# Narrow 4-byte products for the gate weights, a 128-row broadcast of the running maximum, and a layer-2 modulation whose sums are the stationary operand

## The chip, the cores and the metric

One core of one Trainium2 chip runs the whole program. The metric is the device time of one execution in microseconds (us). Engines are named as in the profile: PE is TensorE's matmul side and PEld its weight loads, DVE is VectorE, ACT is ScalarE, POOL is GpSimd, SP is SyncE, which issues the DMAs. PSUM is the accumulator memory, with eight banks.

## What is computed

Two layers over 512 tokens of 1024 channels. Cut to what the change touches:

```
mod = silu(c) @ w_ada[l] + b_ada[l]; shift, scale, gate = split(mod, 3)
h = rms_norm(x, norm_g) * (1 + scale) + shift;   u = h @ w_in
rg_x, rg_z, ml_x, ml_o, ml_z = split(u)
y_rg = rglru(conv(rg_x)) * silu(rg_z)
xc = silu(conv(ml_x)); q = xc @ w_q; k = xc @ w_k; v = ml_x @ w_v      # 4 heads of 256 channels
gates = [q, k, v] @ w_if + b_if      # 3072 x 8: log i and f of 4 heads
s = (q k^T / 16) * exp(d - m_t), causal;  m_t a running maximum over tokens
cell = s v / max(|sum s|, exp(-m_t));    y_ml = norm(sigmoid(ml_o) * cell) * silu(ml_z)
x = x + gate * ([y_rg, y_ml] @ w_out)
```

Everything is in 4-byte floats, and the answer is wanted to that precision.

## The kernel before, in words

**Products.** A large product is made of three: each operand is split into a rounded part (`whi`, `hh`, `xch`, ...; ACT writes it, type fp32r) and the rest (`wlo`, `hl`, `xcl`, ...; DVE writes it), and `mm3` (line 495) adds high x high, high x low and low x high in a PSUM bank. An fp32r product is one record on PE. A product of unsplit 4-byte operands (`f32=True`) is two records of the same shape on PE.

**Order.** The class `Planner` records every instruction and then issues each engine's in the order of a list schedule with its own costs; PE follows the traced order except where an operand isn't there yet in its plan, and then takes a later product. Each engine then runs its list strictly in order. The SBUF tiles come from slots: three for raw weights (`raw`), four each for their two parts (`whi`, `wlo`), 62 others.

**One layer.** First the conv inputs of the heads (`mx`, lines 1199 to 1248), then for each head `qk_weights` (line 781), once `v_gate_weights` (line 801), and `ml_head` (line 838): `p = A x` with `A = w_q w_k^T`, `v`, and the scores `S`. The gates' columns are never made from q, k and v: `w_if` is multiplied into `w_q`, `w_k`, `w_v` beforehand, and the 8 result columns ride along as extra columns of `p` (512 to 520) and of `v` (256 to 264). Then `gate_chain` (line 906) makes the running maximum, and for each head `ml_oz`, `ml_sw` (line 980), `ml_sv`, `ml_yt`; then the RG-LRU half, and `w_out` (`out`, `outq`).

**The gate weights before.** `gate_weights` pads the 8 columns of each block of `w_if` to 32. `qk_weights` runs four unsplit products with the padded block as stationary operand (128 x 32) and 256 columns of raw weights moving, each in another quarter of the array's columns (`tile_position=(0, 32q)`), into one bank `wqg`. `fold` (line 770) copies the bank to SBUF (`wfsb`), transposes and adds the quarters by two unsplit products with a selector (`wfT`), and copies the result (`wf`). `v_gate_weights` does the same with the bank `wvg` for `w_v`, two heads at a time, on raw weights: `w_vT` is not split.

**The modulation of layer 2** (the program's `l = 1`). DVE sums the products over the eight row blocks into `macc` (128 x 1024 in two tiles), in the background. `mod_sum` (line 645) then adds over the 128 rows: four tiled products with a block of ones as stationary operand and 256 columns of `macc` moving (`modps`), a copy (`modsb`), and two products with `sel4` that turn the row into columns (`modT`).

**The maximum.** `mhl` holds the four rows of the running maximum in two parts, in rows 0 to 3 and 32 to 35; `ml_sw` spreads one head's row over 128 partitions by a product with `selh` over 36 rows (`Mbc`).

Of the kernel before, what the change touches and what calls it, by code (L numbers as in the profile page):

```python
# [15 lines left out]
ALU = mybir.AluOpType  # L16
# [14 lines left out]
# columns of the packed per-channel parameters  # L31
# [3 lines left out]
# what of adaLN is summed up on the vector engine: (layer, third)  # L35
# [3 lines left out]
# order of the rows of w_out: the mLSTM half first  # L39
CORD = list(range(8, 16)) + list(range(0, 8))  # L40
# where block j of the causal scores lies: (tile, first column)
# [4 lines left out]
class View:  # L46
    """A part of a logical tile; becomes an access pattern when its instruction is issued."""
# [60 lines left out]
class Planner:  # L108
    """Records instructions, then issues them on each engine in the order of a list schedule: the tensor
    engine follows the traced order, the others serve what it needs first."""  # L110
# [132 lines left out]
    def deadlines(self):  # L243
# [14 lines left out]
        # a PSUM bank is wanted again by a later tile; ready a little ahead of that  # L258
# [27 lines left out]
    def schedule(self):  # L286
# [4 lines left out]
        ready = {e: [] for e in engines}     # (late, i)  # L291
        events = []                          # (time, i): a finished instruction
        nfree = {k: [(0.0, s) for s in range(n)] for k, (n, _) in self.kinds.items()}
        # tiles still without a slot, by the deadline of their first use
# [18 lines left out]
        def fits(o):  # L313
# [4 lines left out]
            for k, bs in need.items():  # L318
                room = len(nfree[k]) - len(bs)
                if room < 0:  # L320
                    return False
                # slots stay for the tiles that come before these
                ahead, w, h, last = 0, want[k], head[k], max(b.first for b in bs)
                while h < len(w) and w[h][0] < last:
                    if w[h][1].slot is None and w[h][1] not in bs:
                        ahead += 1
                        if ahead > room:
                            return False
                    h += 1
            return True  # L330

        def bank_free(o):
            # engines take turns at a PSUM bank
# [24 lines left out]
        while done < len(ops):  # L358
# [23 lines left out]
            # next time at which something changes  # L382
# [43 lines left out]
def trunk_kernel(ctx: ExitStack, tc: tile.TileContext, x, cT, params, bif, bgate, fg,  # L426
# [80 lines left out]
    # t < s: above any maximum, so that its exponential is 0; elsewhere below any  # L507
# [3 lines left out]
    # rows 32 q of four row groups; and pairs of groups, or all, row by row  # L511
    sel4, sel2, selg = keep("sel4", [128, 4]), keep("sel2", [128, 2]), keep("selg", [128, 16])
    sela, selm, selh = keep("sela", [128, 8]), keep("selm", [36, 4]), keep("selh", [36, 4, 128], F32R)

    def selectors():
        P.vcopy(sel4, ident[:, 0:128:32])
        P.tt(sel2, ident[:, 0:128:64], ident[:, 32:128:64], ALU.add)
        for n in range(2):
            P.tt(selg[:, 8 * n:8 * n + 8], ident[:, 64 * n:64 * n + 8], ident[:, 64 * n + 32:64 * n + 40], ALU.add)
        P.tt(sela, selg[:, 0:8], selg[:, 8:16], ALU.add)  # L520
        P.tt(selm, ident[0:36, 0:4], ident[0:36, 32:36], ALU.add)
# [32 lines left out]
    def log1p_exp_neg(ab, shape):  # L554
        # log(1 + exp(-ab)) for ab >= 0: u = exp(-ab), 2 atanh(u / (2 + u))
# [23 lines left out]
    # 4 softplus(-lambda), and halves of the biases of the RG-LRU gates, for both layers  # L579
# [18 lines left out]
    def mod_first(d0, nd):  # L598
        # shift and scale of the first layer, channel blocks d0 .. d0 + nd
# [5 lines left out]
        for k in range(4):  # L605
            # quadrants: (which, half of the rows)
# [25 lines left out]
    def mod_units(l, w):  # L632
        # third w (shift, scale, gate) of layer l: products and sums over the blocks of rows, one step a block
# [11 lines left out]
    def mod_sum(l, w):  # L645
        # the sum over the rows of a block
# [14 lines left out]
        ps = bank("modps", (128, 256))  # L661
        for q in range(4):
            P.mm(ps[32 * q:32 * q + 32, :], ones[:, 0:32], acc[q // 2][:, 256 * (q % 2):256 * (q % 2) + 256], True,
                 True, tp=(0, 32 * q), f32=True)
        sb = slot("modsb", F32, (128, 256))
        P.vcopy(sb, ps)
        pt = bank("modT", (128, 4, 2))
        for c in range(2):
            P.mm(pt[:, :, c], sb[:, 128 * c:128 * c + 128], sel4, True, True, f32=True)
        pt = pt.chan(KC)  # L670
# [32 lines left out]
    def h_part(l, hT, xn, d0, nd, half):  # L703
        # channel blocks d0 .. d0 + nd of two token blocks, transposed, scaled, shifted, split
# [48 lines left out]
    def silu2(ps, name, shape=(128, 512)):  # L753
        # 2 silu
# [6 lines left out]
    def gate_weights(l):  # L761
        raw = slot("wifraw", F32, (128, 24, 8))
        P.dma(raw, w_if[l], 98304)
        pad = [slot("wifpad", F32, (128, 16, 32)), slot("wifpadv", F32, (128, 8, 32))]
        for t, a, b in ((pad[0], 0, 16), (pad[1], 16, 24)):
            P.pool(lambda t=t: nc_g.memset(t.ap(), 0.0), [t], [], 0.4)
            P.vcopy(t[:, :, 0:8], raw[:, a:b, :])
        return pad

    def fold(ps, sel, n):  # L770
        # rows 32 q + g of ps, transposed and summed over the groups q that sel joins: [128, chunk, n]
        sb = slot("wfsb", F32, (128, 256))
        P.vcopy(sb, ps)
        pt = bank("wfT", (128, 2, n))
        for c in range(2):
            P.mm(pt[:, c, :], sb[:, 128 * c:128 * c + 128], sel, True, True, f32=True)
        t = P.tile("gw", (128, 2, n), F32, "wf")
        P.vcopy(t, pt)
        return t

    def qk_weights(l, p, st):
        # A = w_q w_k^T, and the gates' weights seen through w_q and w_k
        raw = load_raw(w_qk[l, p], (2, 2, 256))
        ps = bank("wqg", (128, 256))
        for m in range(2):
            for ec in range(2):
                q = 2 * m + ec
                P.mm(ps[32 * q:32 * q + 32, :], st["pad"][0][:, 8 * m + 2 * p + ec, :], raw[:, m, ec, :], True, True,
                     tp=(0, 32 * q), f32=True)
        hi, lo = load_w(None, (2, 2, 256), raw)  # L790
        pa = bank("A", (128, 2, 256))
        for dc in range(2):
            ds = slice(128 * dc, 128 * dc + 128)
            for ec in range(2):
                mm3(pa[:, dc, :], hi[:, 0, ec, ds], lo[:, 0, ec, ds], hi[:, 1, ec, :], lo[:, 1, ec, :], ec == 0, ec == 1)
        ah, al = slot("Ah", F32R, (128, 2, 256)), slot("Al", F32R, (128, 2, 256))
        split(ah, al, pa)
        st["A"][p] = (ah, al)
        st["gq"][p] = fold(ps, sela, 8)

    def v_gate_weights(l, st):
        for u in range(2):
            raw = load_raw(w_vT[l, u], (2, 2, 256))
            ps = bank("wvg", (128, 256))
            for h in range(2):
                for ec in range(2):
                    q = 2 * h + ec
                    P.mm(ps[32 * q:32 * q + 32, :], st["pad"][1][:, 2 * (2 * u + h) + ec, :], raw[:, h, ec, :],
                         True, True, tp=(0, 32 * q), f32=True)
            st["gv"][u] = fold(ps, selg, 16)  # L810

    def v_weights(l, u, st):
        # w_v of two heads, with the gates' columns beside it
# [581 lines left out]
```

## Time and profile before

| | |
|---|---|
| time, median of 3 runs | 856.05 us (855.46 to 856.55) |
| span of the profiled execution | 853.5 us, 12548 instructions |
| the profiled execution's own time | not listed apart from its span; the median lies 2.5 us above that span |
| PE busy | 835.0 us, 98% |
| DVE, ACT, POOL busy | 607.3, 476.7 and 40.9 us |
| DMA | 107.60 MB, 126 GB/s on the mean |

The span runs from the first to the last instruction of the core. A matmul's busy time overlaps the next one's, so the cost of a matmul in a dense stream is the distance from its start to the next start, not its duration. In the views, "128\*32" is the stationary operand's rows and columns, and "128x256" the moving one.

### The profile page before, as it was taken

The numbers are of one execution on the slowest core, as the hardware profiler recorded it, in microseconds if no ns is written. First come the engines' busy times: TensorE is split into PE (matmuls) and PEld (weight loads), VectorE is DVE, ScalarE is ACT, GpSimd is POOL, SyncE is SP. The second block draws the span as 40 slices with busy tenths as digits, with TensorE's granted clock in tenths as the row PEclk, the third lists the DMA queues.
The fourth block names the chain that finished last, engine by engine and source line by source line (L and its number), as shares of the span: only waits on it lengthen the run. The fifth ranks groups of instructions, "written<-read, shape, count | busy, mean of one in ns | idle before, by whom it ended". The sixth has DMA issues, their size and how long they took to land.

```text
span 853.5 us, 12548 instructions
## 1 busy us (share of the span) xinstructions
PE 835.0 (98%) x4664; PEld 698.1 (82%) x4664; DVE 607.3 (71%) x1227; ACT 476.7 (56%) x938; POOL 40.9 (5%) x66
## 2 busy tenths in 40 slices
PE   4999999999999999999999999999999999999996
PEld 3677897888888888887999789878888888888896
DVE  5467976898889699654466897376775877967643
ACT  4357763655457969622146766364454696893322
POOL 3000001011100000000010000100000000000000
PEclk9999999999999999999999999999999999999999
DMA  9924132466553323523231422033333222273202
GB/s 323 323 81 137 62 121 78 149 202 210 183 195 111 112 74 125 196 99 123 88 107 62 159 87 99 26 111 136 125 109 122 91 77 96 70 252 123 74 26 99
DMA packets 37053, 107.60 MB, mean 126 GB/s; under 512 B 4352, under 2 KB 6400, under 8 KB 36992
## 3 DMA queue, kind: packets, MB, share of 16 engines
q1 hardware_dynamic: 36992, 106.80, 36.2%
q8 instruction: 37, 0.61, 0.3%
q14 instruction: 24, 0.20, 0.1%
HBM read 102.58 MB, written 4.19 MB: 125 GB/s over the span
## 4 chain that ended last, share of the span: by engine, by line
PE 97%; DVE 1%; DMA 1%; POOL 1%; SPq 0%; ACT 0%; issue 0%; POOLq 0%
PE oz L153 20%; PE mx L153 11%; PE outq L153 11%; PE out L153 11%; PE rgz L153 10%; PE rgx L153 10%; PE S L153 4%; PE num L153 3%; PE v L153 3%; PE p L153 3%; PE A L153 2%; PE modps L153 2%; PE px L153 1%; PE pa L153 1%; PE hT L162 1%; PE yT L162 1%
## 5 line engine op out<-in xcount | busy, mean ns | idle before, releaser
L183 ACT CAST whi<-raw 128x1024 fp32r<-128x1024 f32 (+1 forms) x133 | 130.9, 994 | 186.7 <-PE oz L153 63.1
L190 DVE TENSOR_TENSOR wlo<-raw,whi 128x1024 fp32r<-128x1024 f32 (+1 forms) x133 | 151.9, 1148 | 72.4 <-ACT whi L183 72.0
L153 PE MATMUL oz<-whi,hh 128*128 128x512 f32 x256 | 101.8, 399 | 0.0
L153 PE MATMUL oz<-whi,hl 128*128 128x512 f32 x256 | 101.2, 395 | 0.0
L153 PE MATMUL oz<-wlo,hh 128*128 128x512 f32 x256 | 101.1, 395 | 0.0
L153 PE MATMUL outq<-whi,yh 128*128 128x256 f32 x256 | 72.5, 283 | 0.0
L153 PE MATMUL outq<-wlo,yh 128*128 128x256 f32 x256 | 72.4, 283 | 0.0
L153 PE MATMUL outq<-whi,yl 128*128 128x256 f32 x256 | 72.4, 283 | 0.0
L153 PE MATMUL mx<-hh,whi 128*128 128x512 f32 (+1 forms) x166 | 59.1, 358 | 0.0
L153 PE MATMUL mx<-hl,whi 128*128 128x512 f32 (+1 forms) x166 | 58.4, 352 | 0.0
L153 PE MATMUL mx<-hh,wlo 128*128 128x512 f32 (+1 forms) x166 | 57.4, 348 | 0.0
L153 PEld LDWEIGHTS oz<-whi,hh 128*128 128x128 f32 x256 | 48.1, 188 | 11.2 <-issue 1.0
L153 PEld LDWEIGHTS oz<-whi,hl 128*128 128x128 f32 x256 | 48.1, 188 | 11.1
L153 PEld LDWEIGHTS oz<-wlo,hh 128*128 128x128 f32 x256 | 48.1, 188 | 10.2
L153 PE MATMUL out<-whi,yh 128*128 128x512 f32 x128 | 50.6, 396 | 0.0
L153 PE MATMUL out<-whi,yl 128*128 128x512 f32 x128 | 50.6, 395 | 0.0
L153 PE MATMUL rgx<-hh,whi 128*128 128x512 f32 x128 | 50.5, 395 | 0.0
L153 PE MATMUL out<-wlo,yh 128*128 128x512 f32 x128 | 50.5, 394 | 0.0
L153 PE MATMUL rgz<-hh,whi 128*128 128x512 f32 x128 | 50.4, 394 | 0.0
L153 PE MATMUL rgz<-hl,whi 128*128 128x512 f32 x128 | 50.4, 394 | 0.0
L153 PE MATMUL rgx<-hl,whi 128*128 128x512 f32 x128 | 50.4, 394 | 0.0
L153 PE MATMUL rgz<-hh,wlo 128*128 128x512 f32 x128 | 50.4, 394 | 0.0
(256 smaller groups left out, 2029.7 us busy)
## 6 DMA issues: line engine op xcount, KB each, us to landing
raw<-in_w_in_dram SPq DMA_DIRECT2D x45, 512.0 KB, 3.2
raw<-in_w_oz_dram SPq DMA_DIRECT2D x32, 512.0 KB, 3.2
raw<-in_w_ada_dram SPq DMA_DIRECT2D x32, 512.0 KB, 3.3
raw<-in_w_out_dram SPq DMA_DIRECT2D x32, 512.0 KB, 3.2
wada<-in_w_adb_dram SPq DMA_DIRECT2D x24, 256.0 KB, 5.2
x<-in_x_dram SPq DMA_DIRECT2D x16, 256.0 KB, 5.5
raw<-in_w_qk_dram SPq DMA_DIRECT2D x8, 512.0 KB, 3.2
wada<-in_w_ada_dram SPq DMA_DIRECT2D x8, 256.0 KB, 4.3
```

What stands on the lines that cost most here:

```text
L153: self.nc.tensor.matmul(out.ap(), lhsT=lhsT.ap(), rhs=rhs.ap(), start=start, stop=stop, **kw)
L162: self.op("PE", lambda: self.nc.tensor.transpose(out.ap(), in_.ap(), ident.ap()), [out], [in_, ident], 0.109)
L183: self.op("ACT", lambda: self.nc.scalar.copy(out.ap(), in_.ap()), [out], [in_], 0.1 + 0.00084 * in_.n)
L190: self.op(eng, lambda: e.tensor_tensor(out=out.ap(), in0=a.ap(), in1=b.ap(), op=op), [out], [a, b], c)
```

## The change

Three edits; comments are removed as well.

1. **Gate weights.** `w_if` is split into `gatew` (8 high and 8 low columns per block). `qk_weights` puts `gatew`'s columns for `w_q` beside the high part of `w_k` (256 to 272 columns), so that they ride along in the products for `A`, and adds for `w_k` eight narrow products per head: `whi` or `wlo` of `w_k` as stationary 128 x 128 operand and 16 or 8 columns of `gatew` moving. `A` now takes two banks of 272 columns, evacuated one by one. `v_gate_weights` splits `w_vT` into two parts and runs 16 narrow products for each pair of heads. `fold`, its selectors and the padding go.
2. **Layer-2 modulation.** `mod_sum` takes 128 x 128 blocks of `macc` as stationary operand and one column of ones as moving one: eight unsplit products a sum, straight into channel layout.
3. **Maximum.** `selm`, `selh` and `mhl` have 128 rows, and `Mbc` is a product over all of them.

```diff
     def selectors():
-        P.vcopy(sel4, ident[:, 0:128:32])
         P.tt(sel2, ident[:, 0:128:64], ident[:, 32:128:64], ALU.add)
-        for n in range(2):
-            P.tt(selg[:, 8 * n:8 * n + 8], ident[:, 64 * n:64 * n + 8], ident[:, 64 * n + 32:64 * n + 40], ALU.add)
-        P.tt(sela, selg[:, 0:8], selg[:, 8:16], ALU.add)
-        P.tt(selm, ident[0:36, 0:4], ident[0:36, 32:36], ALU.add)
+        P.tt(selm, ident[:, 0:4], ident[:, 32:36], ALU.add)
         P.vcopy(selh, selm.spread(2, 128))
...
     def mod_sum(l, w):
-        ps = bank("modps", (128, 256))
-        for q in range(4):
-            P.mm(ps[32 * q:32 * q + 32, :], ones[:, 0:32], acc[q // 2][:, 256 * (q % 2):256 * (q % 2) + 256], True,
-                 True, tp=(0, 32 * q), f32=True)
-        sb = slot("modsb", F32, (128, 256))
-        P.vcopy(sb, ps)
-        pt = bank("modT", (128, 4, 2))
-        for c in range(2):
-            P.mm(pt[:, :, c], sb[:, 128 * c:128 * c + 128], sel4, True, True, f32=True)
-        pt = pt.chan(KC)
+        pt = bank("modT", (128, KC))
+        for c in range(KC):
+            P.mm(pt[:, c:c + 1], acc[c // 4][:, 128 * (c % 4):128 * (c % 4) + 128], ones[:, 0:1], True, True, f32=True)
...
-    def gate_weights(l):
+    def gate_weights(l, st):
...
+        gw = slot("gatew", F32R, (128, 24, 16))
+        split(gw[:, :, 0:8], gw[:, :, 8:16], raw)
+        st["gw"] = gw
...
     def qk_weights(l, p, st):
         raw = load_raw(w_qk[l, p], (2, 2, 256))
-        ps = bank("wqg", (128, 256))
-        for m in range(2):
-            for ec in range(2):
-                q = 2 * m + ec
-                P.mm(ps[32 * q:32 * q + 32, :], st["pad"][0][:, 8 * m + 2 * p + ec, :], raw[:, m, ec, :], True, True,
-                     tp=(0, 32 * q), f32=True)
-        hi, lo = load_w(None, (2, 2, 256), raw)
-        pa = bank("A", (128, 2, 256))
+        hi = P.tile("whi", (128, 2, 2, 272), F32R, "whi")
+        lo = P.tile("wlo", (128, 2, 2, 256), F32R, "wlo")
+        split(hi[:, :, :, 0:256], lo, raw)
+        gw = st["gw"]
+        P.acopy(hi[:, 1, :, 256:272], gw[:, 2 * p:2 * p + 2, :])
...
         for dc in range(2):
+            pa = bank("A", (128, 272))
             ds = slice(128 * dc, 128 * dc + 128)
             for ec in range(2):
-                mm3(pa[:, dc, :], hi[:, 0, ec, ds], lo[:, 0, ec, ds], hi[:, 1, ec, :], lo[:, 1, ec, :], ec == 0, ec == 1)
-        split(ah, al, pa)
+                P.mm(pa, hi[:, 0, ec, ds], hi[:, 1, ec, :], ec == 0, False)
+                P.mm(pa[:, 0:256], hi[:, 0, ec, ds], lo[:, 1, ec, :], False, False)
+                P.mm(pa[:, 0:264], lo[:, 0, ec, ds], hi[:, 1, ec, 0:264], False, False)
+            for ec in range(2):
+                c = 8 + 2 * p + ec
+                P.mm(pa[:, 256:272], hi[:, 1, ec, ds], gw[:, c, :], False, False)
+                P.mm(pa[:, 256:264], lo[:, 1, ec, ds], gw[:, c, 0:8], False, ec == 1)
+            split(ah[:, dc, :], al[:, dc, :], pa[:, 0:256])
+            P.vcopy(gq[:, dc, :], pa[:, 264:272])
+            P.tt(gq[:, dc, :], gq[:, dc, :], pa[:, 256:264], ALU.add)
-        st["gq"][p] = fold(ps, sela, 8)
+        st["gq"][p] = gq
...
     def v_gate_weights(l, st):
         for u in range(2):
-            raw = load_raw(w_vT[l, u], (2, 2, 256))
-            ps = bank("wvg", (128, 256))
+            wh, wl = load_w(w_vT[l, u], (2, 2, 256))
+            pv = bank("wvg", (128, 2, 2, 16))
             for h in range(2):
-                for ec in range(2):
-                    q = 2 * h + ec
-                    P.mm(ps[32 * q:32 * q + 32, :], st["pad"][1][:, 2 * (2 * u + h) + ec, :], raw[:, h, ec, :],
-                         True, True, tp=(0, 32 * q), f32=True)
-            st["gv"][u] = fold(ps, selg, 16)
+                for dc in range(2):
+                    ds = slice(128 * dc, 128 * dc + 128)
+                    for ec in range(2):
+                        c = 16 + 2 * (2 * u + h) + ec
+                        P.mm(pv[:, dc, h, :], wh[:, h, ec, ds], st["gw"][:, c, :], h + dc + ec == 0, False)
+                        P.mm(pv[:, dc, h, 0:8], wl[:, h, ec, ds], st["gw"][:, c, 0:8], False, h + dc + ec == 3)
+            gv = P.tile("gw", (128, 2, 2, 8), F32, "gv")
+            P.vcopy(gv, pv[:, :, :, 8:16])
+            P.tt(gv, gv, pv[:, :, :, 0:8], ALU.add)
...
-        P.pool(lambda: nc_g.memset(mhl.ap()[0:36, :].bitcast(F32), 0.0), [mhl[0:36, :]], [], 0.3)
+        P.pool(lambda: nc_g.memset(mhl.ap().bitcast(F32), 0.0), [mhl], [], 0.5)
...
-        P.mm(pm, selh[:, h, :], st["mrow"][0:36, :], True, True)
+        P.mm(pm, selh[:, h, :], st["mrow"], True, True)
```

Since the planner decides the order, here are three places as the engines are given it. First PE in layer 1 (`l = 0`), right behind the last `mx` product: `wqg` and `wvg` are the tiled gate products, `A` the products of `w_q w_k^T`, `wfT` the fold. Before:

```order
L153 MATMUL A<-whi 128x256
L153 MATMUL wvg<-raw,wifpadv 32x256
L153 MATMUL A<-wlo,whi 128x256
L153 MATMUL wvg<-raw,wifpadv 32x256
L153 MATMUL A<-whi,wlo 128x256
L153 MATMUL wvg<-raw,wifpadv 32x256 x2
L153 MATMUL wfT<-sela,wfsb 128x8 x2
L153 MATMUL wqg<-raw,wifpad 32x256 x4
```

and now, with `gatew` the split gate columns:

```order
L153 MATMUL A<-whi 128x272
L153 MATMUL A<-wlo,whi 128x256
L153 MATMUL A<-whi,wlo 128x264
L153 MATMUL A<-whi 128x272
L153 MATMUL A<-wlo,whi 128x256
L153 MATMUL A<-whi,wlo 128x264
L153 MATMUL A<-gatew,whi 128x16
L153 MATMUL A<-gatew,wlo 128x8
L153 MATMUL A<-gatew,whi 128x16
L153 MATMUL A<-gatew,wlo 128x8
```

The tiled products that stood between the products for `A` are gone, and the narrow ones follow in runs of four (sixteen for `wvg`), all of them over the whole array.

Second DVE at the same place, with its waits; `mconv`, `msilut`, `xcl` and `xml` lead to the operands of `p` and `v`. Before:

```order
L213 COPY wfsb<-wqg 128x256 [waits PE_49]
L190 TENSOR_TENSOR xml<-xmf,xmh 128x512 [waits Activation_49]
L198 SCALAR_TENSOR_TENSOR msilut<-msilut,mconv 128x512 [waits Activation_49]
L213 COPY wfsb<-wvg 128x256 [waits PE_49]
L213 COPY wf<-wfT 128x16 [waits PE_49]
L198 SCALAR_TENSOR_TENSOR msilut<-msilut,mconv 128x512 [waits Activation_49]
L190 TENSOR_TENSOR Al<-A,Ah 128x512 [waits Activation_49]
```

and now:

```order
L190 TENSOR_TENSOR wlo<-raw,whi 128x1024 [waits DMAHW5_49,PE_49,Activation_49]
L198 SCALAR_TENSOR_TENSOR mconv<-xmf,par,mconv 128x511 [waits Activation_49]
L190 TENSOR_TENSOR wlo<-raw,whi 128x1024 [waits DMAHW6_49,PE_49,Activation_49]
L198 SCALAR_TENSOR_TENSOR mconv<-xmf,par,mconv 128x510 [waits DVE_49]
L198 SCALAR_TENSOR_TENSOR msilut<-msilut,mconv 128x512 [waits Activation_49]
L198 SCALAR_TENSOR_TENSOR mconv<-xmf,par,mconv 128x509 [waits DVE_49]
L190 TENSOR_TENSOR Al<-A,Ah 128x256 [waits Activation_49]
L213 COPY gq<-A 128x8
L190 TENSOR_TENSOR Al<-A,Ah 128x256 [waits Activation_49]
```

The copies that waited for the tiled products have gone from the front of the `msilut` steps, and low halves of whole weight tiles (1024 columns) stand among them.

Third PE in the first of the two modulation sums, under the last `w_out` products. Before:

```order
L153 MATMUL modps<-macc,ones 32x256
L153 MATMUL out<-whi,yh 128x512
L153 MATMUL modps<-macc,ones 32x256 x2
L153 MATMUL out<-wlo,yh 128x512
L153 MATMUL modps<-macc,ones 32x256
L153 MATMUL out<-whi,yl 128x512
```

and now:

```order
L153 MATMUL out<-wlo,yh 128x512
L153 MATMUL out<-whi,yl 128x512
L153 MATMUL modT<-ones,macc 128x1 x8
L153 MATMUL outq<-whi,yh 128x256
L153 MATMUL outq<-wlo,yh 128x256
```

Eight products in one run stand where four tiled ones stood in three places, with the two of `modT` further on.

## Rows read from the trace of the kernel before

**Rows 1.** The profile's page: busy time, share and instructions of each engine, the granted TensorE clock in 40 slices (tenths of full speed, 9 is 90% or more), and the chain that ended last by engine.

```profile
PE 835.0 (98%) x4664; PEld 698.1 (82%) x4664; DVE 607.3 (71%) x1227; ACT 476.7 (56%) x938; POOL 40.9 (5%) x66
...
PEclk9999999999999999999999999999999999999999
...
PE 97%; DVE 1%; DMA 1%; POOL 1%; SPq 0%; ACT 0%; issue 0%; POOLq 0%
```

**Rows 2.** The waits of PE, the longest and the shortest of the four there are: who waited for whom, us in total, times, longest.

```profile
PE modps L153 <- DVE hb L206: 4.5, 1, 4.5
...
PE cumb L153 <- DVE lf L198: 1.1, 1, 1.1
```

**Rows 3.** The timeline of PE at the isolated gate products of head 2 in layer 1: start us, busy us, then engine, line, operation, tiles (x8: eight records).

```profile
84.74 0.28 PE L153 MATMUL S<-ph,xcl 128*128 128x264 f32 x1
84.95 0.64 PE L153 MATMUL wqg<-raw,wifpad 128*32 128x256 f32 x8
85.52 0.39 PE L153 MATMUL A<-whi 128*128 128x256 f32 x1
85.75 0.28 PE L153 MATMUL A<-wlo,whi 128*128 128x256 f32 x1
...
87.53 0.39 PE L153 MATMUL mx<-hh,wlo 128*128 128x512 f32 x1
87.76 0.51 PE L153 MATMUL wfT<-sela,wfsb 128*128 128x8 f32 x4
88.12 0.48 PE L153 MATMUL mx<-hh,whi 128*128 128x512 f32 x1
88.44 0.39 PE L153 MATMUL mx<-hl,whi 128*128 128x512 f32 x1
```

**Rows 4.** The chain of work, two dense pieces, of products of 512 and of 256 columns: start us, length us, what, number of products.

```profile
756.32 39.02 PE out L153 x168
...
801.84 45.26 PE outq L153 x384
```

**Rows 5.** The timeline of PE, first and last row of the gate products in layer 1 (between them 24 products of `A`, the `p` rows at 74.70 (two), 75.26 and 75.85, and 48 gate records) and in layer 2 (12 of `A`, the `mx` rows of 512 columns at 472.72, 473.06, 473.28 and 474.32, and 36 gate records).

```profile
64.47 0.39 PE L153 MATMUL mx<-hh,wlo 128*128 128x512 f32 x1
...
76.17 0.40 PE L153 MATMUL p<-xch,Ah 128*128 128x512 f32 x1
...
465.69 0.28 PE L153 MATMUL mx<-hh,wlo 128*128 128x256 f32 x1
...
474.64 0.39 PE L153 MATMUL mx<-hl,whi 128*128 128x512 f32 x1
```

**Rows 6.** The timeline of PE at a run of six products of 136 columns.

```profile
105.00 0.23 PE L153 MATMUL S<-ph,xch 128*128 128x136 f32 x1
105.06 0.27 PE L153 MATMUL S<-pl,xch 128*128 128x136 f32 x1
...
105.62 0.33 PE L153 MATMUL S<-ph,xch 128*128 128x264 f32 x1
105.79 0.28 PE L153 MATMUL S<-pl,xch 128*128 128x264 f32 x1
```

**Rows 7.** The timeline of PE around the two modulation sums: the first and last row of each stretch (between them, in the first, three more products of 512 and nine of 256 columns that stay; in the second, eleven of 256).

```profile
387.09 0.40 PE L153 MATMUL out<-whi,yl 128*128 128x512 f32 x1
...
391.88 0.27 PE L153 MATMUL outq<-wlo,yh 128*128 128x256 f32 x1
...
401.20 0.28 PE L153 MATMUL outq<-whi,yl 128*128 128x256 f32 x1
...
406.05 0.28 PE L153 MATMUL outq<-whi,yl 128*128 128x256 f32 x1
```

**Rows 8.** The timeline of PE at the first broadcast of the maximum, a product over 36 rows.

```profile
147.61 0.40 PE L153 MATMUL oz<-whi,hl 128*128 128x512 f32 x1
147.94 0.50 PE L153 MATMUL Mbc<-mhl,selh 36*128 36x512 f32 x1
148.36 0.50 PE L153 MATMUL oz<-whi,hh 128*128 128x512 f32 x1
148.70 0.39 PE L153 MATMUL oz<-wlo,hh 128*128 128x512 f32 x1
```

**Rows 9.** Busy time by stretch: us, then PE, PEld, DVE, ACT and POOL busy (instructions), granted clock, DMA share, GB/s.

```profile
64.00:76.00 12.00, 12.00 (x80) 7.36 (x79) 7.50 (x16) 7.90 (x16) 0.10 (x1) 1.00 0.44 136
76.00:108.00 32.00, 32.00 (x200) 28.44 (x201) 30.87 (x57) 25.45 (x66) 0.10 (x1) 1.00 0.23 82
```

**Rows 10.** The timelines of ACT and DVE ahead of and in the first gate stretch; in brackets the idle time before the row and what ended it.

```profile
59.15 1.05 ACT L183 CAST whi<-raw 128x1024 fp32r<-128x1024 f32 x1
...
67.17 0.42 DVE L213 COPY wfsb<-wqg 128x256 f32<-128x256 f32 x1 [1.65 <-PE wqg L153]
...
70.61 0.42 DVE L213 COPY wfsb<-wvg 128x256 f32<-128x256 f32 x1 [1.81 <-PE wvg L153]
71.14 0.17 DVE L213 COPY wf<-wfT 128x16 f32<-128x16 f32 x1
...
71.83 0.68 DVE L190 TENSOR_TENSOR Al<-A,Ah 128x512 fp32r<-128x512 f32 x1
...
78.80 1.22 DVE L190 TENSOR_TENSOR wlo<-raw,whi 128x1024 fp32r<-128x1024 f32 x1
...
80.53 0.41 DVE L190 TENSOR_TENSOR vl<-v,vh 128x256 fp32r<-128x256 f32 x1
```

More of the change, by code (lines that the diff above doesn't have):

```diff
@@ L510, in trunk_kernel @@
                                       fill=1e30, base=0, channel_multiplier=-1), [upper], [upper], 0.3)
-    sel4, sel2, selg = keep("sel4", [128, 4]), keep("sel2", [128, 2]), keep("selg", [128, 16])
-    sela, selm, selh = keep("sela", [128, 8]), keep("selm", [36, 4]), keep("selh", [36, 4, 128], F32R)
+    sel2 = keep("sel2", [128, 2])
+    selm, selh = keep("selm", [128, 4]), keep("selh", [128, 4, 128], F32R)
     def selectors():
-        P.vcopy(sel4, ident[:, 0:128:32])
         P.tt(sel2, ident[:, 0:128:64], ident[:, 32:128:64], ALU.add)
-        for n in range(2):
-            P.tt(selg[:, 8 * n:8 * n + 8], ident[:, 64 * n:64 * n + 8], ident[:, 64 * n + 32:64 * n + 40], ALU.add)
-        P.tt(sela, selg[:, 0:8], selg[:, 8:16], ALU.add)
-        P.tt(selm, ident[0:36, 0:4], ident[0:36, 32:36], ALU.add)
+        P.tt(selm, ident[:, 0:4], ident[:, 32:36], ALU.add)
         P.vcopy(selh, selm.spread(2, 128))
@@ L758, in silu2 @@
         return th
-    def gate_weights(l):
+    def gate_weights(l, st):
         raw = slot("wifraw", F32, (128, 24, 8))
         P.dma(raw, w_if[l], 98304)
[L764 to L779, printed above, removed]
+        gw = slot("gatew", F32R, (128, 24, 16))
+        split(gw[:, :, 0:8], gw[:, :, 8:16], raw)
+        st["gw"] = gw
@@ L792, in qk_weights @@
+        lo = P.tile("wlo", (128, 2, 2, 256), F32R, "wlo")
+        split(hi[:, :, :, 0:256], lo, raw)
+        gw = st["gw"]
+        P.acopy(hi[:, 1, :, 256:272], gw[:, 2 * p:2 * p + 2, :])
+        ah, al = slot("Ah", F32R, (128, 2, 256)), slot("Al", F32R, (128, 2, 256))
+        gq = P.tile("gw", (128, 2, 8), F32, "gq")
         for dc in range(2):
+            pa = bank("A", (128, 272))
             ds = slice(128 * dc, 128 * dc + 128)
             for ec in range(2):
-                mm3(pa[:, dc, :], hi[:, 0, ec, ds], lo[:, 0, ec, ds], hi[:, 1, ec, :], lo[:, 1, ec, :], ec == 0, ec == 1)
@@ L796, in qk_weights @@
-        ah, al = slot("Ah", F32R, (128, 2, 256)), slot("Al", F32R, (128, 2, 256))
-        split(ah, al, pa)
+                P.mm(pa, hi[:, 0, ec, ds], hi[:, 1, ec, :], ec == 0, False)
[5 more added lines that the diff above has]
+                P.mm(pa[:, 256:264], lo[:, 1, ec, ds], gw[:, c, 0:8], False, ec == 1)
@@ L812, in v_weights @@
+            gv = P.tile("gw", (128, 2, 2, 8), F32, "gv")
+            P.vcopy(gv, pv[:, :, :, 8:16])
+            P.tt(gv, gv, pv[:, :, :, 0:8], ALU.add)
+            st["gv"][u] = gv
     def v_weights(l, u, st):
@@ L819, in v_weights @@
         for h in range(2):
-            split(hi[:, h, :, 256:264], lo[:, h, :, 256:264], g[:, :, 8 * h:8 * h + 8])
+            split(hi[:, h, :, 256:264], lo[:, h, :, 256:264], g[:, :, h, :])
         st["wv"] = (hi, lo)
@@ L1243, in trunk_kernel @@
             ml_head_pre(l, p, ps01[p], st)
-        st["pad"] = gate_weights(l)
+        gate_weights(l, st)
         qk_weights(l, 0, st)
```

## The prediction

> **What bounds the kernel now.** I read the page first: PE is busy 98% of the span, the chain that ended last is PE for 97%, and the granted clock is at the upper of its two levels (2.4 GHz) in every slice [rows 1]. Then PE's waits: the longest is 4.5 us, at the start of the program, and the shortest is the gate chain's, 1.1 us [rows 2]; in the stretches that the change touches there is none. So every us of PE's own stream there counts in full, and the work of the others counts only where it makes PE wait. Busy time doesn't price a product, since each overlaps the next; I price by the distance between starts. A dense product costs 39.02 / 168 = 0.232 us with 512 columns and 45.26 / 384 = 0.118 us with 256 [rows 4]; one column more is (0.232 - 0.118) / 256 = 0.45 ns.
>
> **What the removed products cost.** Take an isolated group of four tiled gate products [rows 3]. From the score product ahead of it (84.74) to the second product of A (85.75) are 1.01 us. The two products that stay would take 0.121 (264 columns) and 0.118, so the group costs 0.77 us, though its eight records stand only 0.57 us before the next start: the rest is a late start before it and a slow product behind it. There are five such groups (heads 2 and 3 of layer 1, heads 1 to 3 of layer 2): 3.85 us. An isolated fold lies between two mx products: 0.91 us from 87.53 to 88.44, less two products of 0.232, is 0.446 us [rows 3]; five folds, 2.23 us.
>
> In the first gate stretch of each layer the tiled products alternate with products of A, so I take the whole stretch less what stays. Layer 1: 76.17 - 64.47 = 11.70 us, less five products of 512 columns (1.16) and 24 of A (2.83), is 7.71 us. Layer 2: 474.64 - 465.69 = 8.95 us, less 13 products of 256 columns (1.53) and four of 512 (0.93), is 6.49 us [rows 5]. The gate weights cost PE 3.85 + 2.23 + 7.71 + 6.49 = 20.28 us.
>
> **What the narrow products will cost.** There are 64 for the q and k part and 64 for the v part, with 16 or 8 columns moving and a full 128 x 128 stationary operand. No row of before has this shape in fp32r. The nearest is the run of 136 columns: from 105.00 to 105.79 are 0.79 us for six of them and one of 264 (0.121), so 0.112 us each [rows 6]. The unsplit products of the fold, of 8 columns, give the same: 0.446 / 4 = 0.112 a record [rows 3]. At half and at a sixteenth of 136 columns the price doesn't fall, so it is the stationary operand's, and I take 0.112: 128 x 0.112 = 14.34 us. The wider products of A add 32 x 16 and 32 x 8 columns, 0.34 us. The gate weights thus go from 20.28 to 14.68: **-5.6 us**.
>
> The ends: the first of the run is followed after 0.06 us [rows 6], which would take 0.05 from each. Upward, the product behind a run is late by 0.17 - 0.121 = 0.05 us [rows 6]; I have counted that in, but should a run of four pay it once more, it is 0.013 a product, 1.6 us.
>
> The Trainium skill (TensorEngine Tiling (Array Packing), section When to Use Tiling) advises the opposite of this edit: with few moving columns, swap stationary and moving operand and tile the columns, for up to four times the speed. By that, four tiled products take the time of one, which is the price that the slower rival below gives them, and the gate weights would lose 6.5 us by this edit instead of gaining 5.6; the 0.77 us of the rows speak against it. The same page (section Key Properties) says that changing the tiling mode drains the array, and the gaps of these rows agree with that.
>
> **Modulation of layer 2.** First sum: 391.88 - 387.09 = 4.79 us, less four products of 512 (0.93) and ten of 256 columns (1.18), is 2.68 us. Second: 406.05 - 401.20 = 4.85, less twelve of 256 (1.42), is 3.43 us [rows 7]. In their place come 16 unsplit products, two records each: 32 x 0.112 = 3.58 us. Net **-2.5 us**. They need only the sums that the tiled ones needed too; a copy on DVE goes.
>
> **Maximum.** 148.70 - 147.61 = 1.09 us, less two oz products (0.464), leaves 0.63 us for a product that needs 0.232 in a dense stream [rows 8]. All eight read within 0.01 of that, so it is no wait but what goes with 36 rows. With 128 rows I take the plain 0.232: 8 x 0.395 = **-3.2 us**, and as ends no gain and this one. The memset of 128 rows is POOL's, which is 5% busy, and comes well ahead.
>
> **What it puts on ACT and DVE.** Four more weight tiles are split, 1.05 us on ACT and 1.22 on DVE each [rows 10]. Priced at nothing where it is covered; the cover is thin in layer 1. From 64 to 108 us DVE is busy 7.50 + 30.87 = 38.4 of 44 us [rows 9]. That stretch gets shorter on PE: 7.71 + 0.77 + 0.45 go and 56 narrow products (6.27) and 0.13 of width come, -2.5, so 41.5 us. DVE gets two low halves (2.44), six copies and six additions for gq (12 x 0.17, the copy wf as nearest row), four small ones for gv (0.7) and Al in six halves for three wholes (6 x 0.41 - 3 x 0.68 = 0.4), and loses five wfsb (2.1) and five wf (0.85) [rows 10]: 41.0 of 41.5 us. Between 76 and 108 it ran at 96% and PE never waited [rows 9]; at that share 41.0 needs 42.5, a wait of 1 us. In favour: 3.5 us of DVE's idle time were spent behind the copies of wqg and wvg [rows 10], which go, and in the new order the low halves take that place. The middle is 0.5 us; in layer 2 an mx group follows the v part and gives the time back, so with 0.1 for it I take **+0.6 us**, between 0 and 2.5. Late next would be the xcl that p needs, then xml for v. The A products' second bank, one copy of gate columns on ACT per head and the four selector steps that go at the start (PE waits for data there) I price at nothing.
>
> **Sum:** -5.6 - 2.5 - 3.2 + 0.6 = -10.7 us. The profiled execution's span of 853.5 becomes 842.8; the median lies 2.5 us above that span, so I predict **845.4 us**.
>
> **Rivals.**
> *DVE becomes the bound (0.13).* PE waits for xcl or xml in both layers and the front gains go: up to the 5.6 us of the gate weights, 847 to 850.5 us. For it: the 99% above. Against: layer 2 has 48 mx products behind the v part, and the waiting copies go.
> *Narrow products cost their columns (0.06).* If the stationary operand loads under a neighbour, each costs 0.06 us [rows 6]: 160 x 0.05 = 8 us less, 837 to 842. Against: five of the six in that run cost 0.11. The Trainium skill (TensorE: Matmul & The Clock Gate, section Back-to-back issue gap) gives about 25 ns for up to 64 columns; by it the time would be an estimated 831 us. Its section on LDWEIGHTS counts the 128 columns at 1.2 GHz, 107 ns, and the rows agree with that one.
> *The broadcast doesn't gain (0.05).* If the 0.63 us belong to something else than 36 rows, 3.2 us stay: 848.6 us.
> *Slower (0.02): the gaps are not the tiled products' own.* PE's late starts at 64 to 76 and 465 to 476 us would be operands not yet there, which the tiled products only filled. Removing these then frees no more than their passes: twelve groups and 48 fold records, 12 x 2 x 0.118 + 48 x 0.112 = 8.2 us, and for the modulation 2 x 0.236 + 8 x 0.112 = 1.4 us. What comes is 14.7 and 3.6 us: +8.7, less 3.2 for the maximum, and 0.6, makes 862 us. Beyond the passes I count 20.28 + 6.11 - 9.6 = 16.8 us as the tiled products' own; from the point where under 6.1 us of it (36%) are, the change is slower. Against: five groups among different neighbours cost the same to 0.01 us.
>
> **How the numbers follow.** Forecast 842.5 to 847.0 with 0.72, the rivals as above, 0.02 for anything else. The range leaves out about half of the cheap narrow products, the far end of DVE and the slower case: 842.0 to 849.2. A measurement tells 0.2% (1.7 us) from no change. Only the slower rival, and waits for DVE beyond what I bound, reach 856: faster 0.95, same 0.03, slower 0.02.
>
> **What would show it.** Right: records A<-gatew and wvg<-gatew at 0.11 us from start to start; the first gate stretch of layer 1, from the start of the last mx product to that of the first p, at about 8.5 us; modT in two runs of 1.8 us; Mbc followed by the next product after 0.23; PE waits as before but for under 1 us near p or v of layer 1. Wrong: PE waiting for DVE between 64 and 108 us, narrow products at 0.06, or Mbc still at 0.6.

## The result, and the profile after

The changed kernel takes **850.88 us** (median of 4 runs, 850.69 to 852.13), the kernel before beside it 855.75 us (854.86 to 856.55): a ratio of 0.9947, with an interval of 0.9933 to 0.9961. That is 4.9 us faster, where 10.7 us were forecast; 850.88 lies outside the range of 842.0 to 849.2. The profiled execution took 850.69 us, with a span of 849.0 us.

The page of the changed kernel, the rows that answer to [rows 1]:

```profile
PE 829.3 (98%) x4656; PEld 709.6 (84%) x4656; DVE 608.1 (72%) x1247; ACT 481.6 (57%) x960; POOL 40.3 (5%) x62
...
PEclk9998999999999999999999999999999999999999
...
PE 96%; DVE 1%; POOL 1%; DMA 1%; SPq 0%; issue 0%; ACT 0%; POOLq 0%
```

The thing to see is the one 8 in the row of the clock. A slice is 21.2 us long (849.0 / 40), so this slice, from 63.7 to 84.9 us, holds a stretch at less than full clock. In the second layer the dip is too short to move a digit. The waits of PE, answering to [rows 2] (who waited for whom, us in total, times, longest):

```profile
PE modps L153 <- DMA wada<-in_w_ada_dram: 8.5, 2, 5.0
PE hT L162 <- DVE xn L206: 2.4, 1, 2.4
PE cumb L153 <- DVE lf L198: 2.2, 2, 1.1
```

No wait has come near the gate weights, but cumb now waits in both layers, where before it waited in layer 2 alone. The windows of the changed kernel show the clock (columns as in [rows 9]; the clock is the number behind the engines):

```profile
67.00:71.60 4.60, 4.60 (x43) 4.60 (x42) 4.60 (x12) 4.60 (x11) 0.00 (x0) 1.00 0.57 199
71.60:78.50 6.90, 6.90 (x26) 6.13 (x26) 4.50 (x18) 3.97 (x10) 0.10 (x1) 0.51 0.23 76
78.50:84.00 5.50, 5.50 (x45) 5.34 (x44) 4.56 (x8) 4.63 (x13) 0.10 (x1) 1.00 0.11 33
466.00:470.90 4.90, 4.90 (x43) 4.77 (x42) 3.50 (x5) 4.87 (x8) 0.00 (x0) 1.00 0.55 181
470.90:474.50 3.60, 3.60 (x11) 2.77 (x9) 3.60 (x12) 3.60 (x7) 0.00 (x0) 0.53 0.71 240
```

PE is busy in every us of all five, and yet the clock stands at half, its lower level of 1.2 GHz, in the second and the fifth. By the clock records of the trace the lower level lasts from 71.67 to 78.50 us (6.83 us) in layer 1 and from 471.03 to 474.45 us (3.41 us) in layer 2. The timeline of PE shows what stands ahead of it, and the prices:

```profile
64.90 0.39 PE L153 MATMUL mx<-hh,wlo 128*128 128x512 f32 x1
...
67.04 0.17 PE L153 MATMUL A<-gatew,whi 128*128 128x16 f32 x1
...
70.75 0.26 PE L153 MATMUL wvg<-gatew,whi 128*128 128x16 f32 x1
70.86 0.25 PE L153 MATMUL wvg<-gatew,wlo 128*128 128x8 f32 x1
70.97 0.37 PE L153 MATMUL A<-whi 128*128 128x272 f32 x1
...
71.55 0.30 PE L153 MATMUL A<-wlo,whi 128*128 128x256 f32 x1
71.67 0.40 PE L153 MATMUL A<-whi,wlo 128*128 128x264 f32 x1
...
71.93 0.36 PE L153 MATMUL A<-gatew,wlo 128*128 128x8 f32 x1
72.15 0.36 PE L153 MATMUL A<-gatew,whi 128*128 128x16 f32 x1
...
74.75 0.77 PE L153 MATMUL p<-xch,Ah 128*128 128x512 f32 x1
75.32 0.63 PE L153 MATMUL p<-xcl,Ah 128*128 128x512 f32 x1
75.75 0.63 PE L153 MATMUL p<-xch,Al 128*128 128x512 f32 x1
...
149.72 0.40 PE L153 MATMUL Mbc<-mhl,selh 128*128 128x512 f32 x1
149.96 0.40 PE L153 MATMUL oz<-whi,hh 128*128 128x512 f32 x1
...
388.94 1.84 PE L153 MATMUL modT<-ones,macc 128*128 128x1 f32 x16
390.64 0.36 PE L153 MATMUL outq<-whi,yh 128*128 128x256 f32 x1
```

From 67.04 to 70.97 stand 36 narrow products in one unbroken run (four of `A`, 32 of `wvg`): 3.93 us, 0.109 each. Until there the price is what was forecast. At 71.67 the same kind of product that took 0.28 to 0.30 us of busy time takes 0.40; from there a narrow product stands 0.22 us from the next (71.93 to 72.15) and a 512-column one 0.43 (75.32 to 75.75), where [rows 4] have 0.232. In layer 2 the run of 36 ends at 470.07, and the clock falls at 471.03.

### The profile page after: what moved, and what is told of

Same layout as the page of the kernel before. It is cut to its first block, busy times and chain, and to the rows that moved or that the text cites. A ratio compares the mean times of both kernels' runs of the same rounds, so it can differ in the third digit from the quotient of the medians.

```text
span 849.0 us, 12554 instructions
## 1 busy us (share of the span) xinstructions
PE 829.3 (98%) x4656; PEld 709.6 (84%) x4656; DVE 608.1 (72%) x1247; ACT 481.6 (57%) x960; POOL 40.3 (5%) x62
## 4 chain that ended last, share of the span: by engine, by line
PE 96%; DVE 1%; POOL 1%; DMA 1%; SPq 0%; issue 0%; ACT 0%; POOLq 0%
PE oz L153 19%; PE mx L153 11%; PE outq L153 11%; PE out L153 10%; PE rgz L153 10%; PE rgx L153 10%; PE S L153 4%; PE num L153 3%; PE p L153 3%; PE v L153 3%; PE A L153 2%; PE pa L153 1%; PE px L153 1%; PE modps L153 1%; PE hT L162 1%; POOL u L190 1%
## 5 line engine op out<-in xcount | busy, mean ns | idle before, releaser
L183 ACT CAST whi<-raw 128x1024 fp32r<-128x1024 f32 (+1 forms) x137 | 135.2, 996 | 183.1 <-PE oz L153 66.2
L190 DVE TENSOR_TENSOR wlo<-raw,whi 128x1024 fp32r<-128x1024 f32 (+1 forms) x137 | 156.8, 1150 | 75.0 <-ACT whi L183 74.6
```

The costliest lines, as they stand in the source:

```text
L183: self.op("ACT", lambda: self.nc.scalar.copy(out.ap(), in_.ap()), [out], [in_], 0.1 + 0.00084 * in_.n)
L190: self.op(eng, lambda: e.tensor_tensor(out=out.ap(), in0=a.ap(), in1=b.ap(), op=op), [out], [a, b], c)
```

## Experiments

Two questions were open: what lets the clock fall and what it costs, and where the second wait at cumb comes from. The kernel before ran beside each group of experiments, at 855.21 us (e1 to e4), 855.68 (e5 to e8) and 855.65 (e9, e10).

**e1: the narrow products of v made wide.** Same products, same number, same order and same stationary operands; each streams 128 columns, the 16 gate columns eight times, and only the first copy is read.

```
-  pv = bank("wvg", (128, 2, 2, 16))
+  pv = bank("wvg", (128, 2, 2, 8, 16))
...
+  g = st["gw"][:, c, :].spread(1, 8)
-  P.mm(pv[:, dc, h, :], wh[:, h, ec, ds], st["gw"][:, c, :], ...)
+  P.mm(pv[:, dc, h], wh[:, h, ec, ds], g, ...)
-  P.mm(pv[:, dc, h, 0:8], wl[:, h, ec, ds], st["gw"][:, c, 0:8], ...)
+  P.mm(pv[:, dc, h], wl[:, h, ec, ds], g, ...)
```

> The changed kernel with one difference: each of the 64 narrow products of the v part streams 128 columns (its 16 gate columns read eight times over by a broadcast view, into eight copies in the bank, of which one is used) instead of 16 or 8. Same number of products, same order, same stationary operands, and at 0.112 us a product the stationary operand should still set the pace. Theory A (the runs of 32 narrow products leave the array so little active that TensorE's granted clock falls to its lower level behind them, 71.6 to 78.5 and 471.0 to 474.5 us of the changed kernel): the clock stays at 2.4 GHz in both places and about 3.4 + 1.4 = 4.8 us come back, 846 us. Theory B (the clock is beside the point; PE is held by late operands from DVE and ACT in these stretches): 851 us as the changed kernel, with waits of PE for DVE showing at full clock. Theory C (128 columns are dearer than 16): up to 64 x 0.06 = 3.8 us more, 855 us.

Measured: 846.12 us (845.49 to 846.51), ratio 0.9893, 0.9878 to 0.9909; span 843.8 us. The windows of e1, over the run and behind it, and its timeline:

```profile
66.50:70.50 4.00, 4.00 (x39) 4.00 (x37) 4.00 (x9) 4.00 (x10) 0.00 (x0) 1.00 0.63 229
70.50:78.00 7.50, 7.50 (x53) 6.97 (x52) 7.24 (x25) 6.93 (x17) 0.10 (x1) 1.00 0.22 72
```

```profile
64.36 0.39 PE L153 MATMUL mx<-hh,wlo 128*128 128x512 f32 x1
...
69.80 0.27 PE L153 MATMUL wvg<-gatew,whi 128*128 128x128 f32 x1
69.91 0.27 PE L153 MATMUL wvg<-gatew,wlo 128*128 128x128 f32 x1
...
72.79 0.48 PE L153 MATMUL p<-xch,Ah 128*128 128x512 f32 x1
```

With eight or sixteen times the columns a product costs the same 0.11 us, the engines around it are as full, PE runs the same products in the same order, and the clock stays at its upper level. From the last `mx` to the first `p` of layer 1 are 72.79 - 64.36 = 8.43 us, where 8.5 were forecast; in the changed kernel they are 74.75 - 64.90 = 9.85. Between the two profiled executions lie 849.0 - 843.8 = 5.2 us, and half of the 10.24 us at the lower level (6.83 + 3.41) is 5.1: within 0.1 us the difference is the clock.

**e2: the run cut in two.** The second unit of `v_gate_weights` is called later, in each layer behind the last `ml_head_pre`, so that the runs are of 20 and of 16.

```
-  v_gate_weights(l, st)
+  v_gate_weights(l, st, (0,))
...
   ml_head_pre(l, 3, chan_group(l, 11, hT, ("mx0", "mx1")), st)
+  v_gate_weights(l, st, (1,))
```

> The changed kernel with the v part's 32 narrow products of a layer in two runs of 16: those of heads 0 and 1 where they were, those of heads 2 and 3 behind the mx products of head 3 (layer 1) or likewise behind them in layer 2. No product is added or taken. Theory A (clock): if the run's length matters, the clock falls for a shorter time or not at all, 846 to 849 us; PE waits for nothing more. Theory B (late operands): two of the four extra weight splits move out of the dense stretch of DVE, so it gains too, but with the clock still low behind the runs: 848 to 851 us. What tells them apart is the granted clock beside the time.

Measured: 847.16 us (847.09 to 848.98), ratio 0.9909, 0.9896 to 0.9923; span 845.4 us. The windows of e2, with the first run of 20 in layer 1 (67.73 to 69.88) and in layer 2 (462.73 to 464.88), and behind each:

```profile
66.50:70.00 3.50, 3.50 (x33) 3.50 (x33) 3.50 (x7) 3.50 (x8) 0.00 (x0) 1.00 0.48 150
70.00:77.00 7.00, 7.00 (x49) 6.47 (x49) 6.45 (x23) 6.28 (x15) 0.10 (x1) 1.00 0.24 78
```

```profile
461.50:464.80 3.30, 3.30 (x32) 3.30 (x30) 3.25 (x5) 3.27 (x5) 0.00 (x0) 1.00 0.53 169
464.90:468.30 3.40, 3.40 (x10) 2.72 (x10) 2.67 (x6) 3.40 (x8) 0.00 (x0) 0.50 0.43 140
```

Half the cure: in the profiled execution the fall of layer 1 is gone, that of layer 2 is there with its 3.41 us. In one of the four executions the mean clock was 0.994 and not 0.997, and the time 848.98 us where the others took 847.09 to 847.18. Cutting the run is not a safe remedy, then. Why one run of 20 is followed by a fall and the other isn't, no run here tells. No fall followed a run of 16 in any trace, neither the second runs of e2 nor the modulation's 16 records of one column.

**e3: v's gate weights as before, the rest changed.** `v_gate_weights`, its padded tile and its fold come back from the kernel before; q and k keep the narrow products, in groups of four (once two groups in a row).

> The changed kernel with the v part of the gate weights as it was before (tiled products on raw weights, fold), the q and k part narrow. Theory A: no run of more than 4 narrow products is left, the clock stays up, which gives 4.8 us; the v part costs about 4.6 us a layer (four tiled products in islands among A, four together, two folds) for 3.6, so 2 us are lost: 848 us. Theory B: the four extra weight splits are gone and PE has its operands in time; also faster, with the clock possibly still low at about 72 us. If the clock fell for the four-product runs of the q and k part too, 852 us or more.

Measured: 848.23 us (847.35 to 848.98), ratio 0.9916, 0.9903 to 0.993; no fall of the clock in the middle of the program. The short groups let no fall follow, and even the tiled v is better than the narrow one, which the clock makes dearer than what it replaced.

**e4: the maximum and the modulation alone.** The kernel before with these two edits; all gate weights as before.

> The kernel before with the 128-row broadcast of the maximum and the layer-2 modulation with stationary sums, the gate weights as before. Both theories: the clock stays up, 3.2 + 2.5 = 5.7 us less than before, 850.1 us, so that the gate weights' edit by itself is worth almost nothing in the changed kernel. If one of these two terms was mis-sized, this kernel shows it: 852 us or more.

Measured: 850.46 us (850.29 to 851.82), ratio 0.9945, 0.9933 to 0.9958; no fall, and cumb waits once, as before. This is the changed kernel's own time within what can be told: the gate edit as it was made is worth nothing that can be told, since the clock and the wait at cumb take its gain back. Without the fall it does gain: e1, which has the edit too, is 850.46 - 846.12 = 4.3 us below e4, and with the 1.1 us of the second wait at cumb, which e4 hasn't, that is 5.4, near the 5.6 forecast.

**e7 and e8: the run by itself, elsewhere.** To e4, 36 products that nothing reads are added in one run at the head of the second oz group of layer 1, with 8 columns moving (e7) or 128 (e8).

```
+  if l == 0 and h == 1 and u == 0:
+      for j in range(36):
+          P.mm(ps[0][:, 0:8], hT[j % 8][j // 18][:, 0:128], wh[:, 0, 0:8], True, True)
```

> The kernel of e4_mbc_mod (gate weights as before, 850.46 us, no fall of the clock in the middle), with 36 products more in one run, whose results nothing reads: a 128 x 128 piece of hT as the stationary operand and 8 columns of a weight tile moving, at the head of the second oz group of layer 1, in the dense stretch at about 156 us, far from the gate weights. Theory A (a run of products with few columns by itself lets the clock fall behind it): 36 x 0.112 = 4.0 us for the products, and the clock falls to its lower level right behind them for 3.4 or 6.8 us, which costs half of that: 850.5 + 4.0 + 1.7 or 3.4 = 856.2 or 857.9 us. Theory B (the falls in the changed kernel belong to the gate stretch, where DVE and ACT are full and weights arrive): no fall here, 854.5 us.

> The kernel of e7_run_of_8, but each of the 36 products moves 128 columns and not 8. Theory A (it is the few columns): no fall of the clock, each product still 0.112 us or so, 850.5 + 4.0 = 854.5 us, less than e7 although sixteen times the columns pass. Theory B (the gate stretch): the same 854.5 us as e7, no fall in either. Were it the run as such, whatever its columns: a fall here too, 856.2 us or more.

Measured: e7 858.30 us (857.18 to 858.88), ratio 1.0025, 1.0015 to 1.0035; e8 855.51 us (854.48 to 856.78), ratio 0.9996, 0.9987 to 1.0005. The windows over the run and behind it, of e7 and then of e8:

```profile
156.06:160.45 4.39, 4.39 (x38) 4.38 (x36) 4.39 (x12) 3.39 (x11) 0.00 (x0) 0.89 0.33 107
160.45:166.20 5.75, 5.75 (x15) 4.49 (x16) 4.07 (x7) 1.04 (x1) 0.00 (x0) 0.50 0.67 211
```

```profile
156.90:160.87 3.97, 3.97 (x38) 3.97 (x36) 3.97 (x11) 3.16 (x11) 0.00 (x0) 1.00 0.23 74
160.87:166.60 5.73, 5.73 (x27) 4.66 (x27) 4.35 (x7) 1.28 (x2) 0.00 (x0) 1.00 0.70 232
```

Far from the gate weights, among dense products, the narrow run brings a fall of the same 6.83 us, and the run of 128 columns brings none. By the clock records it begins at 159.52 us, 0.9 us before the run of e7 ends, which is why the window of the run reads 0.89. PE runs the same products in the same order in both. So it is the run and its few columns, not the gate stretch with its full DVE and ACT. A run with sixteen times the columns is 2.8 us cheaper. (e8 came out 1.0 us above its 854.5; its profiled execution starts the first `p` 1.2 us later than that of e4, at the head of the program, where PE waits for data.)

A trace is of one execution; the mean clocks of the others agree. It was 0.991 to 0.993 in all four of the changed kernel and 0.998 or 0.999 in the four of e1; 0.993 to 0.997 in the eight of e7, and 0.997 to 0.999 in the ten of e8, as in the kernel before. The two lowest times of e7 (857.18 and 857.55 us) are the two at 0.997, so the fall was probably shorter there: behind one and the same run it need not be equally long.

The Trainium skill (TensorE: Matmul & The Clock Gate, Part 1: The HAM clock gate) says that the gate follows how busy PE has lately been; the falls that it describes come from waits, and its remedy is to keep PE from idling. Here PE shows no idle time ahead of any of these falls (4.60 us busy of 4.60, 4.90 of 4.90, 4.39 of 4.39), so a busy row isn't enough to go by; the measurement decides.

**The wait at cumb: e5, e6 and e9.** Ahead of cumb runs a chain of small instructions, with a power on GpSimd (`u`) in it. In layer 1 the kernel before has

```profile
132.79 2.90 POOL L190 TENSOR_TENSOR u<-ec,ng 128x16 f32<-128x16 f32 x1 [13.09 <-DVE ng L206]
```

```profile
132.84 1.25 DVE L190 TENSOR_TENSOR wlo<-raw,whi 128x1024 fp32r<-128x1024 f32 x1
```

and the changed kernel

```profile
133.61 3.98 POOL L190 TENSOR_TENSOR u<-ec,ng 128x16 f32<-128x16 f32 x1 [14.89 <-DVE ng L206]
```

```profile
133.60 1.23 DVE L190 TENSOR_TENSOR wlo<-raw,whi 128x1024 fp32r<-128x1024 f32 x1
```

`wlo` is the low half of an oz weight tile, which has nothing to do with the chain. Where it starts 0.05 us behind the power, the power takes 2.90 us; where it starts 0.01 us ahead of it, 3.98. The 1.08 us between them are the wait. To test the order, the chain's -|f| was formed in one DVE instruction and not two, which lets the power start some 0.2 us earlier; in e5 on top of e1, in e6 alone on the kernel before, in both also where the same function serves the start of the program:

```
-  P.stt(ab, fp, -1.0, fp, ALU.mult, ALU.max)
+  P.stt(ab, fp, -1.0, fp, ALU.mult, ALU.min)
...
-  P.ts(ng, ab, -1.0, ALU.mult)
```

> The kernel of e1_wide_v, with one thing more: the gate chain forms -|f| in one VectorE instruction, min(-f, f), where it took the larger of the two and then multiplied by -1. One DVE instruction of 0.17 us less stands ahead of the power on GpSimd, in both layers. In the kernel before the power `u` of layer 1 starts 0.05 us ahead of a low half of a weight tile (`wlo`, 1.25 us, two SBUF inputs) and takes 2.90 us; in layer 2, and in both layers of every kernel with the new gate part, `wlo` starts 0.01 to 0.02 us ahead of the power and the power takes 3.98 us; PE then waits 1.1 us at cumb. Theory A (the one of the two that starts second is held up, so the order decides): the power now starts some 0.2 us ahead of `wlo`, takes 2.9 us in both layers, the two waits of 1.1 us at cumb go, and the time is 846.1 - 2.2 = 843.9 us. Theory B (the longer power has another cause, as how long GpSimd had been idle): it stays at 3.98 us, the chain is shorter by the 0.21 us of the instruction alone, the waits are 0.9 us each, and the time is 845.7 us.

> The kernel before with the one-instruction -|f| alone. Theory A (the order of `wlo` and the power decides): layer 1, where the power was ahead already, keeps 2.9 us and no wait; in layer 2 the power goes from 3.98 to 2.9 us and the wait of 1.1 us at cumb goes: 855.2 - 1.1 = 854.1 us. Theory B (another cause): the power of layer 2 stays at 3.98 us, the wait falls to 0.9 us, and the time is 855.0 us.

Measured: e5 845.67 us (845.29 to 846.66), ratio 0.9881, 0.9867 to 0.9894; e6 856.64 us (855.42 to 857.39), ratio 1.0009, 1.0 to 1.0018. The power takes 2.90 or 2.91 us in both layers of both, so theory A has the mechanism; the times miss it, above all e6, which was to gain 1.1 us. The waits of PE in e5 say why in part; e6 has the same three:

```profile
PE S L153 <- ACT S L176: 0.4, 1, 0.4
PE v L153 <- ACT S L176: 0.4, 1, 0.4
PE cumb L153 <- DVE lf L198: 0.3, 1, 0.3
```

The planner, which counted the chain shorter, put ACT's copies in another order and cumb two oz products earlier in both layers. That brought 0.7 us of waits in layer 1 and 0.4 in layer 2, so e5 still waits 1.1 of e1's 2.2 us, and e6 the same 1.1 as the kernel before. The rest of what e5 and e6 missed lies in no wait of PE and stays open. e9 is e5 with the planner's cost of the one instruction raised by the 0.21 us that were saved (and with the start of the program as it was), so that PE keeps e1's order, but for one product of `v` in each layer that comes one or two places later:

```
+  P.stt(ng, fp, -1.0, fp, ALU.mult, ALU.min)
+  P.ops[-1].cost += 0.21
```

> The kernel of e1_wide_v with -|f| of the gate chain in one VectorE instruction, as in e5_wide_v_min, but its cost in the planner's table raised by 0.21 us, so that the planner counts the chain as long as before and every engine keeps the order of e1 (in e5 the copies of the scores on ACT came in another order, and PE waited 0.4 us twice for them ahead of the chain). Theory A (the power and `wlo`: the one that starts second is held up): the power starts about 0.2 us ahead of `wlo` and takes 2.9 us in both layers, both waits of 1.1 us at cumb go, no new wait comes: 2.2 us under e1 of its time, a ratio of 0.9867 to the kernel before where e1 had 0.9893. Theory B (in e5 it was the new order that made the power short): it stays at 3.98 us, the waits fall to 0.9 us each, ratio 0.989.

Measured: **843.80 us** (843.17 to 844.66), ratio 0.9858, 0.9843 to 0.9873; cumb stands no longer among PE's waits. The power and `wlo` of layer 1 in e9:

```profile
131.54 2.90 POOL L190 TENSOR_TENSOR u<-ec,gng 128x16 f32<-128x16 f32 x1 [14.65 <-DVE gng L198]
```

```profile
131.74 1.23 DVE L190 TENSOR_TENSOR wlo<-raw,whi 128x1024 fp32r<-128x1024 f32 x1 [0.34 <-ACT whi L183]
```

The Trainium skill (SBUF — State Buffer, section SBUF: two separate sides) states a rule that fits: DVE, in an instruction with two SBUF inputs, and GpSimd share a pair of ports as a lock; who starts first gets it and the other blocks. The longer power agrees: it is 1.08 us longer, most of the 1.23 of `wlo`. That the second of the two blocks fully does not show when GpSimd is first: `wlo` then takes 1.23 to 1.25 us, as ever, while the power runs.

**e10: the maximum alone.** The kernel before with the broadcast over 128 rows.

> The kernel before with the maximum's broadcast over 128 rows alone. If the 0.63 us that a broadcast takes in the kernel before belong to its 36 rows: 8 x (0.63 - 0.23 to 0.28) = 2.8 to 3.2 us less, 852.4 us. If they belong to something else, as the change of the stationary operand's source: 855.6 us. The rest of e4_mbc_mod's gain of 4.75 us would be the modulation's: 2.5 us by the rows, 1.6 to 1.9 us by this difference in the first case.

Measured: 852.78 us (851.79 to 853.45), ratio 0.9964, 0.9951 to 0.9976: 2.9 us (855.65 - 852.78), so the gain is the 36 rows'. With e4's 4.75 us, 1.9 are left for the modulation; the intervals of the two runs are too wide to size it so, but their traces do: from the first `out` product of layer 1 to the last `outq` are 93.18 us in e10, as before, and 90.63 in e4, 2.5 less.

## Why the prediction was wrong

**The step that failed** is the price of the narrow products. It took 0.112 us each from rows at the full clock, with [rows 1] showing that clock in every slice, and priced nothing behind a run of them. At the full clock the price holds: in e1 the 128 products cost 14.3 us, forecast 14.34 (though of the prediction's "half and a sixteenth of 136 columns" the rows have only the 8 columns, none has half). In the changed kernel they cost 15.6, since two groups of four of layer 1 fall into the slow stretch; of the 5.2 us between e1 and the changed kernel that leaves 3.9 for the dense products behind the runs. No row of before could price it, since the longest run of 16 columns or fewer there was one of eight records (`wfT`, 473.51 to 474.21 us); but for that reason the term needed an upper bound, and the one that it got for a run, 1.6 us (0.013 a product), was the pipeline's alone.

**The modulation** was right: 1.70 us stand from the 16 records' start at 388.94 to the next product at 390.64, and 0.08 more by which that next one holds up the one behind it. Both sums cost 3.57 us in this way, forecast 3.58.

**The maximum** was right in kind and 0.2 us too good. In all eight places the next product starts 0.23 us behind the broadcast, as forecast. But the 0.395 us were saved in only four of them: in the second pair of each layer eight transposes (`yT`, 128 columns) follow it, and from the start of the `oz` product ahead of it to that of the second one behind the transposes it went from 1.91 to 1.57 us, 0.35 less. Whether all eight cost 0.63 before, as the prediction read them, depends on the price that one gives the transposes. All eight saved 3.0 us, forecast 3.2.

**DVE's +0.6 us** did not come. DVE and ACT are busy 4.60 of 4.60 us in the window of 67.00, and PE waits for neither at `p` or `v`, nor does it in e1, where no slow clock gives them time; an engine that is full but not late costs nothing.

**The second wait at cumb**, 1.1 us, was in no term. The prediction named cumb's wait of [rows 2] and did not ask why only one layer had it; that layer 1 was spared by 0.05 us stood in the trace of before.

The sum with these sizes: -5.6 for the gate weights at the full clock, -2.5 and -3.0 for modulation and maximum, +5.2 for the clock, +1.1 for cumb: -4.8 us, where 4.9 were measured. None of the rivals is what happened: they asked what a product costs and whom PE waits for, and none asked what the products do to PE itself.

## What to carry to other kernels

A product that is cheap by its columns is not priced by its own row alone: where an edit puts tens of them in one unbroken run, look at the granted clock of the stretch behind the run, and bound the cost by what stands there at half speed. Widening the products to a size that costs no more time, here 128 columns, took that loss away in all three places that were tried; shortening the run to 20 did so in one of two. And where the same chain waits in one place and not in another, find out why before forecasting that the change leaves it alone: here 0.05 us between two starts were worth 1.1.

## What the runs showed of the hardware

- The granted clock fell to its lower level in all three places with a run of 36 products of 8 or 16 columns (for 6.83, 3.41 and 6.83 us), 0.7 and 1.0 us behind the run or 0.9 before its end, while PE was busy throughout. In no trace did it fall at a run of as many products where 36, or all but four, had 128 columns.
- Two unrelated instructions, a power on GpSimd and a subtraction of two SBUF tiles on DVE, make the power take 2.90 or 3.98 us, by which starts first; 0.01 us ahead is enough.
